# Sparse attention with screened rows: the stages of a pair given steps of their own, and the screening scores issued twice

## The chip, the cores and the metric

The kernel runs on one core of one Trainium2 chip. A core has five engines with instruction streams of their own: PE (TensorE, matmuls; its weight loads are shown apart as PEld), DVE (VectorE), ACT (ScalarE), POOL (GpSimd) and SP (SyncE, which here only issues transfers). The metric is the time of one execution in device microseconds (us). "Clock" is the mean share of full speed that was granted to TensorE; the records know only 0.5 and 1.0. They begin with the first change of the clock; what comes before it is counted and printed as full speed, though it ran at half. (In the kernel before, until 31.4 us, the transposes of k start 213 ns apart; just after it, 109 ns.) So every mean clock here is a little too high: the 0.684 of before would be 0.65. A run is called slow when it is over 1.5% above the fastest run of the same kernel.

## The reference, cut to what matters

```python
# Q, K, V: (8, 12, 512, 64) float32; threshold = 0.1
scores  = np.einsum('bhqd,bhkd->bhqk', Q, K) / sqrt(64)
weights = softmax(scores)                          # max-subtracted, + 1e-10 in the sum
weights = np.where(weights > threshold, weights, 0)
weights = weights / (np.sum(weights, axis=-1, keepdims=True) + 1e-10)
return np.einsum('bhqk,bhkd->bhqd', weights, V)
```

With random data few rows have any weight above 0.1; all other output rows are zero. So the kernel screens every row cheaply in bf16, then computes exactly only rows that may pass.

## The kernel before

Two heads make a pair, and there are 48 pairs. The screening of a pair takes four steps, one for each block of 128 query rows; a step is numbered g, and `hp, qi = divmod(g, 4)`. The work of one pair, by engine:

- Transpose q and k on PE (fp32; PE writes into PSUM, a small memory of its own, from which the others copy), copy out on ACT, centre the keys on DVE.
- Four times: screening scores on PE (two heads, one matmul each), a row maximum on DVE for one head and a sum of exponentials on ACT for the other (in one of the four, the sum on ACT for both).
- Flag the rows (DVE), rank them by matmuls with a triangle of ones (PE), make slot keys (DVE), turn these into row indices (PE), gather the selected query rows (DVE adds an offset, POOL issues).
- For the selected 128 slots: split the two heads' rows (DVE), transpose them (PE), fp32 scores (PE), exponential (ACT), mask (DVE), transpose the mask (PE), copy it out (DVE), multiply by V (PE), normalise (DVE, ACT), scatter to the output (POOL). The output was filled with zeros before (SP).

The score matmul and the schedule of before:

```python
def do_qk(g):
    hp, qi = divmod(g, SO)
    for h2 in range(2):
        sc = spsum.tile([P, SO * P], f32)
        ps = slice(h2 * D, (h2 + 1) * D)          # head 0: rows 0-63, head 1: rows 64-127
        keep(nc.tensor.matmul(sc[:], lhsT=qk_t[hp][ps, 0, qi * P:(qi + 1) * P],
                              rhs=qk_t[hp][ps, 1, :], start=True, stop=True))
        sc_t[g, h2] = sc
# ...
for g in range((NP + 5) * SO):
    hp, qi = divmod(g, SO)
    # ... loads
    if g < G:
        do_qk(g)
    # ... qi == 0 and qi == 1 cut
    elif qi == 2:
        if has(hp - 1):
            do_idx(hp - 1)
        if g < G:
            do_screen(g)
        if has(hp - 1):
            do_gather(hp - 1)
        if has(nxt):
            do_kcentre(nxt)
        if has(hp - 3):
            do_xmask(hp - 3)
        if has(hp - 2):
            do_split(hp - 2)          # DVE, last in its step ...
        # ...
    else:
        if has(hp - 2):
            do_xtr(hp - 2)            # ... and PE needs it first in the next
        # ...
```

Every instruction keeps the order in which the program writes it, within its engine (`keep`). So a stage that stands early on one engine, and needs something late on another, stops the whole stream behind it.

The softmax here doesn't subtract the row's maximum and nothing guards it: scores larger than these inputs give would overflow.

Of the kernel before, what the change touches and what calls it, by code (L numbers as in the profile page):

```python
# [11 lines left out]
def kernel(  # L12
# [26 lines left out]
    nc = tc.nc  # L39
# [95 lines left out]
    nc.gpsimd.memset(cuts[:, 1, 0:SO - 1], CUT * CS / scale)  # L135
# [12 lines left out]
    ptpsum = ctx.enter_context(tc.tile_pool(name="ptpsum", bufs=1, space=bass.MemoryType.PSUM))  # L148
    mpsum = ctx.enter_context(tc.tile_pool(name="mpsum", bufs=2, space=bass.MemoryType.PSUM))
# [8 lines left out]
    qb_t, sq_t, nm_t = {}, {}, {}  # L158
# [25 lines left out]
    def do_qev(hp, sc):  # L184
        qk = tpool.tile([P, 2, SO * P], SCREEN)
        keep(nc.scalar.copy(qk[:, 0, :], sc[:]))  # L186
        qk_t[hp] = qk

    def do_kev(hp, sc):
        kt = ktpool.tile([P, SO * P], f32)  # L190
        ksum = small.tile([P, 1], f32)
        keep(nc.scalar.activation(kt[:], sc[:], ACTF.Copy, accum_out=ksum[:]))  # L192
        k_t[hp] = kt
        ks_t[hp] = ksum
# [12 lines left out]
    def do_norms(hp):  # L207
        nm = mpsum.tile([P, P], f32, name="sm")
        sq = sq_t.pop(hp)
        for which in range(2):  # L210
            for r in range(SO):
                c = (which * SO + r) * 2
                keep(nc.tensor.matmul(nm[:, c:c + 2], lhsT=sq[:, which, r * P:(r + 1) * P], rhs=heads[:],
                                      start=True, stop=True))
        nm_t[hp] = nm
# [6 lines left out]
    def do_qk(g):  # L222
        hp, qi = divmod(g, SO)
        for h2 in range(2):
            sc = spsum.tile([P, SO * P], f32)
            ps = slice(h2 * D, (h2 + 1) * D)
            keep(nc.tensor.matmul(sc[:], lhsT=qk_t[hp][ps, 0, qi * P:(qi + 1) * P],  # L227
                                  rhs=qk_t[hp][ps, 1, :], start=True, stop=True))
            sc_t[g, h2] = sc

    def do_screen(g):
# [5 lines left out]
        for h2 in range(2):  # L237
            sc = sc_t.pop((g, h2))
            if h2 == 0 or qi == SO - 1:
# [12 lines left out]
    def do_rank(hp):  # L252
        f = f_t[hp]
        rk = mpsum.tile([P, P], f32, name="sm")
# [18 lines left out]
    def do_idx(hp):  # L273
        oh = oh_t.pop(hp)[:].rearrange("p h s r -> p r (h s)")
        ix = mpsum.tile([P, P], f32, name="sm")
# [23 lines left out]
    def do_xtr(hp):  # L299
        xp = mpsum.tile([P, P], f32, name="sm")  # L300
# [29 lines left out]
    def do_xpt(hp):  # L330
        m = m_t.pop(hp)
        pt = ptpsum.tile([P, SO, P], bf16)
# [10 lines left out]
    def do_xpv(hp):  # L343
        pt, v_bf = pts_t.pop(hp), v_in.pop(hp)
        o = mpsum.tile([P, P], f32, name="sm")
# [10 lines left out]
    def do_xout(hp):  # L356
        o = o_t.pop(hp)
        rcp = small.tile([P, 1], f32)
        keep(nc.vector.tensor_scalar_add(rcp[:], o[:, D:D + 1], 1e-10))
        keep(nc.vector.reciprocal(rcp[:], rcp[:]))  # L360
        res = outp.tile([P, D], f32)
        keep(nc.scalar.activation(res[:], o[:, 0:D], ACTF.Copy, scale=rcp[:, 0:1]))  # L362
        keep(nc.gpsimd.indirect_dma_start(  # L363
            out=Or, out_offset=bass.IndirectOffsetOnAxis(ap=ix_t.pop(hp)[:, 0:1], axis=0),
            in_=res[:], in_offset=None, element_offset=hp * 2 * S * D, bounds_check=2 * S - 1, oob_is_err=False))
# [6 lines left out]
    do_qev(0, do_tr(q_in.pop(0)))  # L372
    do_kev(0, do_tr(k_in.pop(0)))
# [4 lines left out]
    def has(hp):  # L378
        return 0 <= hp < NP

    for g in range((NP + 5) * SO):
        hp, qi = divmod(g, SO)
        nxt = hp + 1
        if qi == 0 and has(hp + PRE):
            do_load(hp + PRE)
        if g < G:
            do_qk(g)
        if qi == 0:
            if has(hp - 1):
                do_flags(hp - 1)  # L390
                do_rank(hp - 1)
            if has(nxt):
                tr = do_tr(q_in.pop(nxt))
            if has(hp - 3):
                do_xqk(hp - 3)
            if g < G:
                do_screen(g)
            if has(nxt):
                do_qev(nxt, tr)
            if has(hp - 4):  # L400
                do_xptev(hp - 4)
            if has(hp):
                do_squares(hp)
        elif qi == 1:
            if has(nxt):
                tr = do_tr(k_in.pop(nxt))
            if has(hp - 4):
                do_xpv(hp - 4)
            if g < G:
                do_screen(g)  # L410
            if has(hp - 1):
                do_key(hp - 1)
            if has(nxt):
                do_kev(nxt, tr)
            if has(hp - 3):
                do_xexp(hp - 3)
        elif qi == 2:
            if has(hp - 1):
                do_idx(hp - 1)
            if g < G:  # L420
                do_screen(g)
            if has(hp - 1):
                do_gather(hp - 1)
            if has(nxt):
                do_kcentre(nxt)
            if has(hp - 3):
                do_xmask(hp - 3)
            if has(hp - 2):
                do_split(hp - 2)
            if has(hp - 4):  # L430
                do_xout(hp - 4)
        else:
            if has(hp - 2):
                do_xtr(hp - 2)
            if has(hp - 3):
                do_xpt(hp - 3)
            if has(hp):
                do_norms(hp)
            if has(hp + 2):
                do_vload(hp + 2)  # L440
            if g < G:
                do_screen(g)
            if has(hp - 2):
                do_xev(hp - 2)
            if has(hp):
                do_normev(hp)
# [10 lines left out]
    over_t = mpsum.tile([P, P], f32, name="sm")  # L457
# [9 lines left out]
    with tc.If(many > 0):  # L467
        with tc.For_i(0, NP, 1) as hp:
# [9 lines left out]
            for qi in range(SO):  # L478
                for h2 in range(2):
# [12 lines left out]
                    pt_ps = ptpsum.tile([P, SO, P], bf16, name="pt")  # L492
# [5 lines left out]
                    o = mpsum.tile([P, P], f32, name="sm")  # L498
# [47 lines left out]
```

## Time and profile before

| kernel before | |
|---|---|
| median of 4 runs | 483.32 us (480.74 to 484.42) |
| profiled span | 483.1 us |
| from the first screening scores to the end of the last | 8.2 to 453.6 us: 9.28 us a pair |
| mean distance of pairs 5 to 45 | 9.56 us |
| mean clock | 0.684 |

The first part of the page gives each engine's busy time:

```profile
PE 355.0 (73%) x2450; PEld 182.8 (38%) x2450; DVE 259.6 (54%) x729; ACT 261.3 (54%) x865; POOL 140.3 (29%) x172
```

No engine is near full, though PE, at 73%, looks like the one to watch. But part of that is the low clock: the same matmul is counted as longer. The view of windows over one pair (columns: window, its length, then busy time and instruction count of PE, PEld, DVE, ACT and POOL, the granted clock, the transfers' share, GB/s) says it for a pair that ran mostly at full clock:

```profile
69.00:78.30 9.30, 6.76 (x54) 3.15 (x53) 5.34 (x15) 5.30 (x18) 2.82 (x3) 0.87 0.53 117
```

Even there PE is idle 2.5 of 9.3 us.

### The profile page before, as it was taken

The page shows a single profiled execution, that of the slowest core. Times are in us where ns is not written, and L with a number is a line of the kernel's source. Part 1 is how long each engine was busy: PE and PEld are TensorE (multiplying, and loading weights), DVE is VectorE, ACT ScalarE, POOL GpSimd, SP SyncE. Part 2 cuts the span into 40 slices and gives each one's busy share as a digit, 9 for nine tenths or more (in the row PEclk, how much of TensorE's full clock was granted, in tenths as well). Part 3 has the DMA queues.
Part 4 walks back from the last instruction along what each step waited for, and adds up shares of the span by engine and source line. Part 5 has one row for each costly group of instructions (what it writes and reads, how often), then busy time and mean ns, then how long its engine had stood idle before and what let it go on. Part 6 is the DMA issues. An engine that isn't in the chain of part 4 may idle for free. (4 is left out here: it accounts for less than half of the span.)

```text
span 483.1 us, 7777 instructions
## 1 busy us (share of the span) xinstructions
PE 355.0 (73%) x2450; PEld 182.8 (38%) x2450; DVE 259.6 (54%) x729; ACT 261.3 (54%) x865; POOL 140.3 (29%) x172
## 2 busy tenths in 40 slices
PE   3878876887788678867886787688768867886861
PEld 2444333433434343434343433344343434343330
DVE  2565465556555654565456555555555565556540
ACT  3675465555645564556455556555565556564520
POOL 5122223223322332233223322432242233223221
PEclk9996667666766676677667666766676667666555
DMA  7994544454344435443544445445434441311000
GB/s 161 234 230 90 127 107 91 88 117 108 83 94 117 102 81 105 108 103 80 118 96 100 88 88 127 93 90 122 97 87 95 119 100 39 67 15 13 6 3 7
DMA packets 124461, 45.87 MB, mean 95 GB/s; under 512 B 104758, under 2 KB 118272, under 8 KB 124416
## 3 DMA queue, kind: packets, MB, share of 16 engines
q1 hardware_dynamic: 108288, 37.76, 30.3%
q0 software_dynamic: 16128, 7.57, 12.9%
q8 instruction: 21, 0.34, 0.3%
q14 instruction: 24, 0.20, 0.1%
HBM read 39.32 MB, written 14.16 MB: 111 GB/s over the span
## 5 line engine op out<-in xcount | busy, mean ns | idle before, releaser
L241 ACT ACTIVATE junk<-sc 128x512 bf16<-128x512 f32 x240 | 143.9, 603 | 77.5 <-PE sc L227 77.4
L244 DVE TENSOR_REDUCE stat<-sc 128x1 f32<-128x512 f32 x144 | 99.1, 688 | 123.0 <-PE sc L227 122.1
L284 POOL DMA_INDIRECT qsel<-in_Q_dram,idx x48 | 50.9, 1060 | 278.2 <-DVE idx L283 253.8
L227 PE MATMUL sc<-qk 64*128 64x512 bf16 x384 | 99.9, 515 | 2.0 <-DVE qk L197 1.8
L312 PE MATMUL sc<-kt,xq 128*128 128x512 f32 x96 | 91.6, 1058 | 0.0
L301 PE MATMUL sm<-identity_f,qb 128*128 128x128 f32 x48 | 18.4, 384 | 83.0 <-DVE qb L294 83.0
L363 POOL DMA_INDIRECT out_dram<-res,idx x48 | 48.9, 1019 | 54.7 <-ACT res L362 47.6
L362 ACT ACTIVATE res<-sm,rcp 128x64 f32<-128x64 f32 x48 | 15.1, 314 | 79.5 <-DVE rcp L360 72.9
L180 PE MATMUL sc<-identity_f,q_sb 128*128 128x128 f32 x192 | 49.4, 408 | 5.1 <-POOL heads L130 4.6
L241 ACT ACTIVATION_READ_ACCUMULATOR junk<-sc 128x1 f32 x240 | 50.6, 211 | 0.0
L180 PE MATMUL sc<-identity_f,k_sb 128*128 128x128 f32 x192 | 49.2, 406 | 2.0 <-DMA k_sb<-in_K_dram 1.9
L227 PEld LDWEIGHTS <-qk 64*128 64x128 bf16 x384 | 19.5, 98 | 73.4 <-issue 71.3
L186 ACT CAST qk<-sc 128x512 bf16<-128x512 f32 x48 | 28.1, 586 | 33.0 <-PE sc L180 33.0
L248 DVE TENSOR_TENSOR f<-stat,cuts 128x8 bf16<-128x8 f32 x48 | 8.0, 167 | 70.2 <-ACT junk L241 69.3
L301 PEld LDWEIGHTS sm<-identity_f,qb 128*128 128x128 f32 x48 | 7.3, 152 | 99.1 <-DVE qb L294 99.1
L180 PEld LDWEIGHTS sc<-identity_f,k_sb 128*128 128x128 f32 x192 | 31.7, 202 | 21.1 <-issue 21.1
L167 POOL DMA_DIRECT2D v_bf<-in_V_dram x48 | 37.4, 779 | 1.2 <-issue 1.2
L326 DVE SCALAR_TENSOR_TENSOR m<-e,tv 128x512 bf16<-128x512 f32 x48 | 36.1, 751 | 1.7
L192 ACT ACTIVATE kt<-sc 128x512 f32<-128x512 f32 x48 | 28.6, 596 | 13.9 <-PE sc L180 13.9
L180 PEld LDWEIGHTS sc<-identity_f,q_sb 128*128 128x128 f32 x192 | 32.0, 204 | 5.6 <-POOL heads L130 4.6
L204 DVE TENSOR_TENSOR sq<-qk 128x1024 bf16<-128x1024 bf16 x48 | 32.6, 679 | 0.0
L318 ACT ACTIVATE e<-sc 128x512 f32<-128x512 f32 x48 | 28.4, 593 | 6.6 <-PE sc L312 6.6
(64 smaller groups left out, 384.5 us busy)
## 6 DMA issues: line engine op xcount, KB each, us to landing
q_sb<-in_Q_dram SPq DMA_DIRECT2D x96, 128.0 KB, 3.2
k_sb<-in_K_dram SPq DMA_DIRECT2D x96, 128.0 KB, 2.9
out_dram<-zero SPq DMA_DIRECT2D x48, 256.0 KB, 3.1
v_bf<-in_V_dram POOLq DMA_DIRECT2D x48, 128.0 KB, 3.2
qsel<-in_Q_dram,idx POOLq DMA_INDIRECT x48, 2.5
out_dram<-res,idx POOLq DMA_INDIRECT x48, 2.2
```

The source lines that it names most:

```text
L167: keep(nc.gpsimd.dma_start(out=v_bf[:], in_=Vf[hp]))
L180: keep(nc.tensor.matmul(sc[:, r * P:(r + 1) * P], lhsT=src[:, r, :], rhs=identity_f32[:], is_transpose=True, start=True, stop=True))
L192: keep(nc.scalar.activation(kt[:], sc[:], ACTF.Copy, accum_out=ksum[:]))
L204: keep(nc.vector.tensor_tensor(out=sq[:], in0=qk[:], in1=qk[:], op=ALU.mult))
L227: keep(nc.tensor.matmul(sc[:], lhsT=qk_t[hp][ps, 0, qi * P:(qi + 1) * P], rhs=qk_t[hp][ps, 1, :], start=True, stop=True))
L241: keep(nc.scalar.activation(junk[:], sc[:], ACTF.Exp, scale=BETA * scale / CS, accum_out=stat[:, h2, qi:qi + 1]))
L244: keep(nc.vector.tensor_reduce(stat[:, h2, qi:qi + 1], sc[:], axis=AX.X, op=ALU.max))
L284: keep(nc.gpsimd.indirect_dma_start(out=qsel_bufs[hp % NS][:], out_offset=None, in_=Qr, in_offset=bass.IndirectOffsetOnAxis(ap=idx[:, 0:1] ...
L312: keep(nc.tensor.matmul(sc[:], lhsT=xq_t.pop(hp)[:], rhs=k_t.pop(hp)[:], start=True, stop=True))
L318: keep(nc.scalar.activation(e[:], xs_t.pop(hp)[:], ACTF.Exp, scale=scale, accum_out=sum1[:]))
L326: keep(nc.vector.scalar_tensor_tensor(out=m[:], in0=e[:], scalar=tv[:, 0:1], in1=e[:], op0=ALU.is_gt, op1=ALU.mult))
L363: keep(nc.gpsimd.indirect_dma_start(out=Or, out_offset=bass.IndirectOffsetOnAxis(ap=ix_t.pop(hp)[:, 0:1], axis=0), in_=res[:], in_offset=N ...
```

## The change

The intent was twofold. First, a pair's stages get steps of their own, so that PE never meets a stage in the same step as the stage that feeds it. Second, the screening scores are computed twice into the same buffer: the second copy writes the same numbers, and is there to keep TensorE busy enough for its full clock. The core of the diff:

```diff
@@ do_qk
-            keep(nc.tensor.matmul(sc[:], lhsT=qk_t[hp][ps, 0, qi * P:(qi + 1) * P],
-                                  rhs=qk_t[hp][ps, 1, :], start=True, stop=True))
+
+            for _ in range(2):
+                keep(nc.tensor.matmul(sc[:], lhsT=qk_t[hp][ps, 0, qi * P:(qi + 1) * P],
+                                      rhs=qk_t[hp][ps, 1, :], start=True, stop=True))
             sc_t[g, h2] = sc
@@ the loop
-    for g in range((NP + 5) * SO):
...          (the four branches by qi are gone)
+    PLAN = {
+        "pe": {-4: [do_ktr], -3: [do_qtr], 1: [do_norms], 5: [do_rank], 7: [do_idx], 12: [do_xtr],
+               14: [do_xqk], 18: [do_xpt], 20: [do_xpv]},
+        "act": {-4: [do_kev], -3: [do_qev], 2: [do_normev], 12: [do_xev], 15: [do_xexp], 21: [do_xout]},
+        "dve": {-2: [do_kcentre], 0: [do_squares], 4: [do_flags], 6: [do_key], 8: [do_gather],
+                11: [do_split], 17: [do_xmask], 19: [do_xptev], 21: [do_xrcp]},
+    }
+    LAST = 22
+
+    def run(engine, g):
+        for t in sorted(PLAN[engine], reverse=True):
+            hp, at = divmod(g - t, SO)
+            if at == 0 and 0 <= hp < NP and (hp > 0 or t >= 0):
+                for step in PLAN[engine][t]:
+                    step(hp)
+
+    for g in range(G + LAST):
...          (loads cut)
+        if g < G:
+            do_qk(g)
+        run("pe", g)
+        if g < G:
+            do_screen(g)
+        run("dve", g)
+        run("act", g)
```

A key of the plan is a step counted from the pair's first screening. Within a step the oldest pair's stage comes first (`reverse=True`). Beside that, the transposed mask's PSUM buffer joins the small PSUM pool (three shared buffers in place of two and one), k is transposed before q, and one of the four steps' exponential and maximum change places.

More of the change, by code (lines that the diff above doesn't have):

```diff
@@ L134 @@
     nc.gpsimd.memset(cuts[:], CUT_SUM)
-    nc.gpsimd.memset(cuts[:, 1, 0:SO - 1], CUT * CS / scale)
+    nc.gpsimd.memset(cuts[:, 1, :], CUT * CS / scale)
+    nc.gpsimd.memset(cuts[:, 1, 2:3], CUT_SUM)
     NS = 3
@@ L147 @@
     spsum = ctx.enter_context(tc.tile_pool(name="spsum", bufs=5, space=bass.MemoryType.PSUM))
-    ptpsum = ctx.enter_context(tc.tile_pool(name="ptpsum", bufs=1, space=bass.MemoryType.PSUM))
-    mpsum = ctx.enter_context(tc.tile_pool(name="mpsum", bufs=2, space=bass.MemoryType.PSUM))
+    mpsum = ctx.enter_context(tc.tile_pool(name="mpsum", bufs=3, space=bass.MemoryType.PSUM))
     junkp = ctx.enter_context(tc.tile_pool(name="junk", bufs=2))
@@ L157 @@
     xp_t, xq_t, xs_t, e_t, m_t, s_t, ptp_t, pts_t, o_t = {}, {}, {}, {}, {}, {}, {}, {}, {}
-    qb_t, sq_t, nm_t = {}, {}, {}
+    qb_t, sq_t, nm_t, rc_t, tr_t = {}, {}, {}, {}, {}
     def load_pair(q_sb, k_sb, hp):
@@ L182, in do_tr, with do_qtr, do_ktr, do_qev @@
         return sc
-    def do_qev(hp, sc):
+    def do_qtr(hp):
+        tr_t[hp, "q"] = do_tr(q_in.pop(hp))
+    def do_ktr(hp):
+        tr_t[hp, "k"] = do_tr(k_in.pop(hp))
+    def do_qev(hp):
+        sc = tr_t.pop((hp, "q"))
         qk = tpool.tile([P, 2, SO * P], SCREEN)
+        qk_t[hp] = qk
         keep(nc.scalar.copy(qk[:, 0, :], sc[:]))
-        qk_t[hp] = qk
-    def do_kev(hp, sc):
+    def do_kev(hp):
+        sc = tr_t.pop((hp, "k"))
         kt = ktpool.tile([P, SO * P], f32)
@@ L207, in do_norms @@
     def do_norms(hp):
-        nm = mpsum.tile([P, P], f32, name="sm")
+        nm = mpsum.tile([P, P], f32, name="sm", tag="sm")
         sq = sq_t.pop(hp)
@@ L238, in do_screen @@
             sc = sc_t.pop((g, h2))
-            if h2 == 0 or qi == SO - 1:
+            if h2 == 0 or qi == 2:
                 junk = junkp.tile([P, SO * P], bf16)
@@ L253, in do_rank @@
         f = f_t[hp]
-        rk = mpsum.tile([P, P], f32, name="sm")
+        rk = mpsum.tile([P, P], f32, name="sm", tag="sm")
         cnt = rk[:, 0:2 * SO].rearrange("p (h r) -> p h r", h=2)
@@ L274, in do_idx @@
         oh = oh_t.pop(hp)[:].rearrange("p h s r -> p r (h s)")
-        ix = mpsum.tile([P, P], f32, name="sm")
+        ix = mpsum.tile([P, P], f32, name="sm", tag="sm")
         for r in range(SO):
@@ L299, in do_xtr @@
     def do_xtr(hp):
-        xp = mpsum.tile([P, P], f32, name="sm")
+        xp = mpsum.tile([P, P], f32, name="sm", tag="sm")
         keep(nc.tensor.matmul(xp[:], lhsT=qb_t.pop(hp)[:].rearrange("p h d -> p (h d)"), rhs=identity_f32[:],
@@ L331, in do_xpt @@
         m = m_t.pop(hp)
-        pt = ptpsum.tile([P, SO, P], bf16)
+        sm = mpsum.tile([P, SO, P], bf16, name="smt", tag="sm")
+        pt = sm
         for kj in range(SO):
@@ L344, in do_xpv @@
         pt, v_bf = pts_t.pop(hp), v_in.pop(hp)
-        o = mpsum.tile([P, P], f32, name="sm")
+        o = mpsum.tile([P, P], f32, name="sm", tag="sm")
         for h2 in range(2):
@@ L354, in do_xpv, with do_xrcp @@
         o_t[hp] = o
-    def do_xout(hp):
-        o = o_t.pop(hp)
+    def do_xrcp(hp):
+        o = o_t[hp]
         rcp = small.tile([P, 1], f32)
@@ L360, in do_xout @@
         keep(nc.vector.reciprocal(rcp[:], rcp[:]))
+        rc_t[hp] = rcp
+    def do_xout(hp):
         res = outp.tile([P, D], f32)
-        keep(nc.scalar.activation(res[:], o[:, 0:D], ACTF.Copy, scale=rcp[:, 0:1]))
+        keep(nc.scalar.activation(res[:], o_t.pop(hp)[:, 0:D], ACTF.Copy, scale=rc_t.pop(hp)[:, 0:1]))
         keep(nc.gpsimd.indirect_dma_start(
             out=Or, out_offset=bass.IndirectOffsetOnAxis(ap=ix_t.pop(hp)[:, 0:1], axis=0),
-            in_=res[:], in_offset=None, element_offset=hp * 2 * S * D, bounds_check=2 * S - 1, oob_is_err=False))
+            in_=res[:], in_offset=None, element_offset=hp * 2 * S * D,
+            bounds_check=2 * S - 1, oob_is_err=False))
     PRE = 3
@@ L371 @@
         do_vload(hp)
-    do_qev(0, do_tr(q_in.pop(0)))
-    do_kev(0, do_tr(k_in.pop(0)))
+    do_ktr(0)
+    do_kev(0)
+    do_qtr(0)
+    do_qev(0)
     do_kcentre(0)
     G = NP * SO
-    def has(hp):
-        return 0 <= hp < NP
-    for g in range((NP + 5) * SO):
+    PLAN = {
[5 more added lines that the diff above has]
+    }
@@ L382 @@
+    LAST = 22
[6 more added lines that the diff above has]
+    for g in range(G + LAST):
         hp, qi = divmod(g, SO)
-        nxt = hp + 1
-        if qi == 0 and has(hp + PRE):
+        if qi == 0 and PRE <= hp + PRE < NP:
             do_load(hp + PRE)
+        if qi == 3 and hp + 2 < NP:
+            do_vload(hp + 2)
@@ L386 @@
         if g < G:
             do_qk(g)
-        if qi == 0:
-            if has(hp - 1):
-                do_flags(hp - 1)
-                do_rank(hp - 1)
-            if has(nxt):
-                tr = do_tr(q_in.pop(nxt))
-            if has(hp - 3):
-                do_xqk(hp - 3)
-            if g < G:
-                do_screen(g)
-            if has(nxt):
-                do_qev(nxt, tr)
-            if has(hp - 4):
-                do_xptev(hp - 4)
-            if has(hp):
-                do_squares(hp)
-        elif qi == 1:
-            if has(nxt):
-                tr = do_tr(k_in.pop(nxt))
-            if has(hp - 4):
-                do_xpv(hp - 4)
-            if g < G:
-                do_screen(g)
-            if has(hp - 1):
-                do_key(hp - 1)
-            if has(nxt):
-                do_kev(nxt, tr)
-            if has(hp - 3):
-                do_xexp(hp - 3)
-        elif qi == 2:
-            if has(hp - 1):
-                do_idx(hp - 1)
-            if g < G:
-                do_screen(g)
-            if has(hp - 1):
-                do_gather(hp - 1)
-            if has(nxt):
-                do_kcentre(nxt)
-            if has(hp - 3):
-                do_xmask(hp - 3)
-            if has(hp - 2):
-                do_split(hp - 2)
-            if has(hp - 4):
-                do_xout(hp - 4)
-        else:
-            if has(hp - 2):
-                do_xtr(hp - 2)
-            if has(hp - 3):
-                do_xpt(hp - 3)
-            if has(hp):
-                do_norms(hp)
-            if has(hp + 2):
-                do_vload(hp + 2)
-            if g < G:
-                do_screen(g)
-            if has(hp - 2):
-                do_xev(hp - 2)
-            if has(hp):
-                do_normev(hp)
@@ L456 @@
     nc.vector.tensor_reduce(over[:], most[:], axis=AX.X, op=ALU.max)
-    over_t = mpsum.tile([P, P], f32, name="sm")
+    over_t = mpsum.tile([P, P], f32, name="sm", tag="sm")
     nc.tensor.matmul(over_t[0:1, :], lhsT=over[:], rhs=identity_f32[:], start=True, stop=True)
@@ L491 @@
                                                    op0=ALU.is_gt, op1=ALU.mult)
-                    pt_ps = ptpsum.tile([P, SO, P], bf16, name="pt")
+                    pt_ps = mpsum.tile([P, SO, P], bf16, name="smt", tag="sm")
                     for kj in range(SO):
@@ L497 @@
                     nc.scalar.copy(pt[:], pt_ps[:])
-                    o = mpsum.tile([P, P], f32, name="sm")
+                    o = mpsum.tile([P, P], f32, name="sm", tag="sm")
                     for kj in range(SO):
```

## The prediction

> **What bounds the kernel now.** I read the page first, its forty slices and its groups:
>
> ```profile
> PE   3878876887788678867886787688768867886861
> ...
> PEclk9996667666766676677667666766676667666555
> ...
> L244 DVE TENSOR_REDUCE stat<-sc 128x1 f32<-128x512 f32 x144 | 99.1, 688 | 123.0 <-PE sc L227 122.1
> ...
> L227 PE MATMUL sc<-qk 64*128 64x512 bf16 x384 | 99.9, 515 | 2.0 <-DVE qk L197 1.8
> ...
> L301 PE MATMUL sm<-identity_f,qb 128*128 128x128 f32 x48 | 18.4, 384 | 83.0 <-DVE qb L294 83.0
> ```
>
> No engine is full: PE is busy 355 of 483 us (7.4 us for each of 48 pairs), VectorE 260 (5.4) and ScalarE 261 (5.4). VectorE's longest wait, 122 us, is for PE's scores; PE's longest, 83 us, is for VectorE (48 times 1.7 us, in front of the selected rows' transpose). So the engines wait for each other in turn, and PE runs at two thirds of its clock. The first full screening starts at 8.2 us and the last near 455 in the timeline: a pair takes (455 - 8.2)/48 = 9.3 us, and 28 us are tail.
>
> Next the timeline of PE alone, over a stretch in which the clock was full (until 75.8):
>
> ```profile
> 69.18 0.39 PE L227 MATMUL sc<-qk 64*128 64x512 bf16 x2
> 69.50 0.66 PE L180 MATMUL sc<-identity_f,k_sb 128*128 128x128 f32 x4
> 70.09 0.33 PE L349 MATMUL sm<-v_bf,pt 128*64 128x64 bf16 x8
> 70.35 0.25 PE L352 MATMUL sm<-ones_bf,pt 128*128 128x1 bf16 x4
> 70.53 0.39 PE L227 MATMUL sc<-qk 64*128 64x512 bf16 x2
> 70.91 0.29 PE L277 MATMUL sm<-row_no,oh 128*128 128x1 f16 x4
> 71.14 0.39 PE L227 MATMUL sc<-qk 64*128 64x512 bf16 x2
> 73.30 0.33 PE L301 MATMUL sm<-identity_f,qb 128*128 128x128 f32 x1 [1.78 <-DVE qb L294]
> 73.47 0.39 PE L334 MATMUL pt<-identity_bf,m 128*128 128x128 bf16 x4
> 73.92 0.34 PE L213 MATMUL sm<-heads,sq 128*128 128x2 bf16 x8
> 74.19 0.39 PE L227 MATMUL sc<-qk 64*128 64x512 bf16 x2
> 75.28 0.18 PE L256 MATMUL sm<-f,tri 128*128 128x8 bf16 x1 [0.70 <-ACT norms L218]
> 75.32 0.21 PE L258 MATMUL sm<-f,ones_bf 128*128 128x6 bf16 x3
> 75.39 0.73 PE L180 MATMUL sc<-identity_f,q_sb 128*128 128x128 f32 x4
> ```
>
> Columns: start, length, work, and in brackets PE's idle time and who ended it. Two stops of 1.8 and 0.7 us stand in each pair, because one step holds both a stage and the stage it needs (on VectorE the split waits behind four other stages of its own step). They also cost the clock, as the windows of 3.41 us show:
>
> ```profile
> 58.73:62.14 3.41, 3.41 (x24) 1.52 (x24) 1.19 (x3) 1.80 (x6) 0.00 (x0) 0.50 0.65 168
> 62.14:65.56 3.42, 1.80 (x21) 1.20 (x20) 2.46 (x8) 1.56 (x8) 1.28 (x2) 0.50 0.37 80
> 65.56:68.97 3.41, 3.07 (x13) 1.40 (x12) 1.69 (x4) 2.05 (x8) 1.55 (x2) 0.50 0.32 41
> 68.97:72.38 3.41, 2.56 (x27) 1.30 (x26) 2.54 (x8) 2.42 (x8) 0.30 (x1) 1.00 0.71 190
> 72.38:75.79 3.41, 1.72 (x23) 1.28 (x24) 1.84 (x7) 2.24 (x9) 2.38 (x3) 1.00 0.21 48
> ```
>
> The second number is PE's busy time, the third from the end the granted clock. A window with PE busy throughout (58.73) did not raise the clock of the next; one with 3.07 us (65.56) did. So busy time is not what decides. I counted columns streamed instead (a scores pair in two row halves as 512, a 128-column fp32 transpose as 256, since they stand 0.109 us apart, the fp32 scores of selected rows as 4 x 512). Over all windows of the trace, cold ones above about 3150 columns are followed by a full clock and those below are not; full-clock windows with 3300 or more stay, those with 2130 or less fall. A pair has 7300 such columns, some 2700 for each window of 9.3 us of pair: just too few, so the clock goes up and down once in each pair.
>
> **What the Trainium skill says.** "TensorE: Matmul & The Clock Gate", Part 1 (The HAM clock gate): PE is throttled to half its clock unless a free-running window of about 3.4 us was busy. The trace agrees: the granted share is only ever 0.5 or 1.0, in stretches of 3.413 us or multiples. Part 2 there (Back-to-back issue gap) gives N/2.4 + 2.5 ns for a matmul of N columns warm and N/1.2 ns cold: 0.216 and 0.427 us for 512. Part 3 (Packing small matmuls) says that matmuls on different row groups overlap; here the two heads of a scores pair, in rows 0-63 and 64-127, take 0.39 us together, as long as one. Part 4 (PE-mode transpose) says that transposes do not count as busy for the gate; my count fits the trace only with them in, so I go by the trace.
>
> **The change part by part.** (1) The stages of a pair get steps of their own, each a step or more after what feeds it; the order of the built program confirms it, and VectorE's and ScalarE's instructions are the same in number and size (one reduction and one exponential change places). Gone are PE's stops before the split rows' transpose (1.7 us) and before the rank (0.3 to 0.7).
> (2) Each scores matmul is issued twice. The order on PE is head 0, head 0, head 1, head 1. The second of head 0 needs the same rows as the first, so waits 0.213 us; the first of head 1 overlaps it; the second of head 1 comes 0.213 later. A step costs 0.43 us more at full clock, 1.7 us a pair (0.85 and 3.4 at half).
> (3) PSUM: the transposes' own buffer joins the small pool, three shared instead of two and one; still five score buffers.
>
> PE's work of a pair at full clock, from start to next start above: scores 4 x (0.32 + 0.43) = 3.0; two transpose groups 2 x 0.59 = 1.18; selected scores half of their cold 1.85 = 0.93 (estimate); selected transposes 0.17 + 0.30; weights by V 0.26 + 0.18; norms 0.27; rank 0.11; index 0.23. Sum 6.6 us. VectorE needs 5.4, ScalarE 5.4. So PE is the bound if its clock is full, and the work is hidden behind it.
>
> What waits are left? I laid the steps out by the built waits. Step 1 holds on VectorE: reduce (scores end 0.81 after the step starts, +0.06 semaphore, 0.69), two reciprocal parts 0.31, threshold 0.17, mask 0.75: mask ready at 2.8. PE has by then done step 1 (scores 0.75, rank 0.11, norms 0.27, transposes 0.59) and step 2's scores (0.75) = 2.5, and waits 0.3 for the mask. Step 3: reduce and copy of the transposed mask end at 2.0; PE gets there at 0.98 + 0.75 = 1.7, waits 0.3. The score buffers come free a step ahead. Pair: 6.6 + 0.6 = 7.2; I add 0.3 for waits not seen, 7.5.
>
> The clock: a pair has 9500 columns now even with a half-row matmul as 256; in 7.5 us that is 4300 for each window, and the thinnest stretch (steps 3 and 0) still has 3800, over the 3300 that held. At half clock a pair would take some 11.7 us with 2760 on average, but the windows with the selected scores reach 3200 and more, so it gets warm in the first pairs that have all stages, and stays.
>
> Time: 8.2 + 48 x 7.5 + 28 (the tail is the same chain, with a few steps more in name) = 396; 2 for the cold start: **398 us**, 0.83 of the time before.
>
> **The rivals.** (a) *The clock stays low or falls often.* Then doubled scores are pure cost: 11.7 us a pair, 600 us. For it: only a count of columns says otherwise, and half-row matmuls could count for less. Against: every window count above. 5 in 100. (b) *The doubled matmuls don't overlap* (head 1 waits for both of head 0): 0.21 more a step, 8.3 a pair, 435 us. Against: the 4 ns between the heads' starts today. (c) *The output's queues become the bound.* A scatter waits for a zero fill to land and the next fill for that scatter: POOL 1.0 + landing 2.2 + issue 0.6 + landing 3.1 = 6.9 us a round, and the index of a later pair waits for the scatter's buffer. Hidden at 9.3 us, it is close to 7.5; with landings of 4 us, 8 us a pair, 420. (d) *VectorE and ScalarE turn out the bound* at 5.4 each: this would need PE's 6.6 to be too high; with no waits at all 6.6 gives 355.
>
> **Range and chances.** The spread of (b), (c) and a clock lost now and then is upward, that of no waits downward: 375 to 435. Faster by over 2% 0.93; within 2% 0.03; slower 0.04, nearly all of it (a).
>
> **What would show it.** Right: granted clock over 0.9 from about 50 us to the last scores; the scores group 768 matmuls, four in about 0.8 us; a pair in 7.2 to 7.8 us; PE's wait before the split rows' transpose gone, and its longest waits 0.3 us on the mask and the copied transposes. Wrong: a clock of 0.5 in long stretches (a); four scores in 1.0 us (b); PE, VectorE or POOL waiting for fills or scatters in each pair (c); PE idle over 1 us a pair on anything else.

## The result, and the profile after

| | before | after |
|---|---|---|
| median (range), 4 runs each | 483.32 us (480.74 to 484.42) | 352.38 us (351.61 to 353.02) |
| ratio of fast runs, 95% interval | | 0.7296 (0.7260 to 0.7332) |
| clock of the profiled run | 0.684 | 0.961 |
| mean distance of pairs 5 to 45 | 9.56 us | 6.58 us |
| before the first scores, after the last | 8, 30 us | 9, 28 us |

A ratio here is the mean time of one kernel's fast runs over that of the other's of the same rounds, so it is not quite the ratio of the medians. The changed kernel is 27% faster; the predicted 398 us and its range of 375 to 435 were both too high.

The page of the kernel after, first its busy times, PE's slices and the clock:

```profile
PE 284.2 (81%) x2834; PEld 135.5 (39%) x2834; DVE 262.9 (75%) x729; ACT 259.1 (74%) x865; POOL 154.9 (44%) x173
...
PE   2698988888888988888988888888888888887650
...
PEclk9998999999999999999999999999999999999655
```

PE issues 384 more matmuls (2834 against 2450) and is still busy 71 us less, because the clock record now shows full speed from 33.3 to 326.8 us without a break. DVE and ACT have the busy time they had, in a span 132 us shorter. Next the groups that answer to those of before (columns: line, engine, operation, output from inputs, shapes, count; busy us, mean ns of one; idle time just before them and who ended it):

```profile
L237 PE MATMUL sc<-qk 64*128 64x512 bf16 x768 | 118.6, 385 | 0.7 <-ACT qk L194 0.7
...
L345 PE MATMUL smt<-identity_bf,m 128*128 128x128 bf16 x192 | 19.7, 227 | 26.5 <-DVE m L336 26.0
...
L360 PE MATMUL sm<-v_bf,pt 128*64 128x64 bf16 x384 | 16.1, 205 | 17.9 <-DVE pt L351 17.9
```

The scores take 118.6 us busy for 768 where 384 took 99.9. In the listing that keeps shapes apart, the selected rows' transpose, which had waited 83 us for the split rows, waits almost nothing:

```profile
L311 PE MATMUL sm<-identity_f,qb 128*128 128x128 f32 x48 | 15.1, 315 | 1.7 <-DVE qb L304 1.7
```

PE's longest waits are now for the mask (L336) and for the copy of the transposed mask (L351). The timeline of PE over one pair, from one mask's transposes to the next:

```profile
150.11 0.40 PE L345 MATMUL smt<-identity_bf,m 128*128 128x128 bf16 x4 [0.50 <-DVE m L336]
150.34 1.08 PE L322 MATMUL sc<-kt,xq 128*128 128x512 f32 x2
151.35 0.61 PE L237 MATMUL sc<-qk 64*128 64x512 bf16 x4
151.89 0.29 PE L287 MATMUL sm<-row_no,oh 128*128 128x1 f16 x4
152.12 0.61 PE L237 MATMUL sc<-qk 64*128 64x512 bf16 x4
153.11 0.33 PE L360 MATMUL sm<-v_bf,pt 128*64 128x64 bf16 x8 [0.38 <-DVE pt L351]
...
153.63 0.60 PE L180 MATMUL sc<-identity_f,k_sb 128*128 128x128 f32 x4
154.16 0.61 PE L237 MATMUL sc<-qk 64*128 64x512 bf16 x4
...
155.58 0.61 PE L237 MATMUL sc<-qk 64*128 64x512 bf16 x4
156.69 0.40 PE L345 MATMUL smt<-identity_bf,m 128*128 128x128 bf16 x4 [0.50 <-DVE m L336]
```

Two things are to be seen. From the mask's transposes at 150.11 to the next at 156.69 a pair takes 6.58 us, with two waits in it. And a step's four score matmuls stand 0.54 us from what follows them (151.35 to 151.89), not the 0.75 us that the prediction had worked out. The windows view of a stretch of one whole period, 6.58 us, around the same pair:

```profile
149.97:156.55 6.58, 5.70 (x59) 2.72 (x59) 5.45 (x16) 5.34 (x20) 3.17 (x4) 1.00 0.70 148
```

PE is busy 5.70 us and idle 0.88, which is the two waits of the timeline, 0.50 and 0.38.

**Why a step costs 0.54.** The single records of the step at 151.35 settle it. The program issues head 0 twice, then head 1 twice. In the trace the four start at 0, 7, 226 and 233 ns, and last 386, 386, 376 and 376 ns. The second to start carries the wait for ScalarE, which only head 1's first matmul has; the two that start last carry the semaphore updates, which only each head's second copy has. So the first copy of head 1 ran beside the first copy of head 0, ahead of head 0's second copy, which stands before it in the program. At half clock, in the first step at 9.05 us, the same pattern shows with 401 ns between the two couples. The doubling thus costs one matmul's time a step, 0.22 us, and not two. Nor did the compiler put the copies in that order: in most steps head 1 starts 3 to 4 ns after head 0 where one copy of head 0 stands before it in the program (the kernel before, and experiment 4), 6 to 7 ns with two copies and 10 ns with three (experiment 3). It comes up later by some 3 ns for each copy written ahead of it, and passes those that have to wait. Three of the 192 steps, all before 27 us, did start in the written order.

### The profile page after: what moved, and what is told of

It is laid out like the page before. It is cut to its first block, busy times and chain, and to the rows that moved or that the text cites. A ratio compares the mean times of both kernels' runs of the same rounds, so it can differ in the third digit from the quotient of the medians.

```text
span 350.6 us, 8644 instructions
## 1 busy us (share of the span) xinstructions
PE 284.2 (81%) x2834; PEld 135.5 (39%) x2834; DVE 262.9 (75%) x729; ACT 259.1 (74%) x865; POOL 154.9 (44%) x173
## 5 line engine op out<-in xcount | busy, mean ns | idle before, releaser
L294 POOL DMA_INDIRECT qsel<-in_Q_dram,idx x48 | 62.1, 1294 | 139.3 <-DVE f L258 124.6
L237 PE MATMUL sc<-qk 64*128 64x512 bf16 x768 | 118.6, 385 | 0.7 <-ACT qk L194 0.7
L322 PE MATMUL sc<-kt,xq 128*128 128x512 f32 x96 | 54.4, 650 | 0.0
L345 PE MATMUL smt<-identity_bf,m 128*128 128x128 bf16 x192 | 19.7, 227 | 26.5 <-DVE m L336 26.0
L336 DVE SCALAR_TENSOR_TENSOR m<-e,tv 128x512 bf16<-128x512 f32 x48 | 36.1, 752 | 1.7
L180 PE MATMUL sc<-identity_f,k_sb 128*128 128x128 f32 x192 | 29.9, 280 | 9.0 <-DMA k_sb<-in_K_dram 9.0
L205 DVE TENSOR_SCALAR qk<-kt,ksum 128x512 bf16<-128x512 f32 x48 | 30.3, 632 | 6.7 <-ACT kt L200 6.7
L180 PE MATMUL sc<-identity_f,q_sb 128*128 128x128 f32 x192 | 31.8, 290 | 0.0
L360 PE MATMUL sm<-v_bf,pt 128*64 128x64 bf16 x384 | 16.1, 205 | 17.9 <-DVE pt L351 17.9
L345 PEld LDWEIGHTS <-m 128*128 128x128 bf16 x192 | 11.2, 99 | 48.9 <-DVE m L336 47.9
L360 PEld LDWEIGHTS <-pt 128*64 128x64 bf16 x384 | 10.6, 113 | 42.5 <-DVE pt L351 39.5
```

The lines of the kernel that those rows point to most:

```text
L180: keep(nc.tensor.matmul(sc[:, r * P:(r + 1) * P], lhsT=src[:, r, :], rhs=identity_f32[:], is_transpose=True, start=True, stop=True))
L205: keep(nc.vector.tensor_scalar(qk_t[hp][:, 1, :], k_t[hp][:], CS, ks_t.pop(hp)[:, 0:1], op0=ALU.mult, op1=ALU.subtract))
L294: keep(nc.gpsimd.indirect_dma_start(out=qsel_bufs[hp % NS][:], out_offset=None, in_=Qr, in_offset=bass.IndirectOffsetOnAxis(ap=idx[:, 0:1] ...
L322: keep(nc.tensor.matmul(sc[:], lhsT=xq_t.pop(hp)[:], rhs=k_t.pop(hp)[:], start=True, stop=True))
L336: keep(nc.vector.scalar_tensor_tensor(out=m[:], in0=e[:], scalar=tv[:, 0:1], in1=e[:], op0=ALU.is_gt, op1=ALU.mult))
L345: keep(nc.tensor.matmul(pt[:, kj, :], lhsT=m[:, kj * P:(kj + 1) * P], rhs=identity_bf[:], is_transpose=True, start=True, stop=True))
```

## The experiments

The theory after the result: the plan brings nearly all of the gain, by removing PE's stops and by that lifting the clock; the doubling costs 0.22 us a step, since the two heads' matmuls run beside each other copy by copy, and the miss of the prediction is that 0.22 for 0.43. The rivals: that the plan alone falls back to a low clock and the doubling is what lifts it; that the heads do run in series and something else became shorter; and that the output's round of scatter and zero fill sets the pair. All twelve kernels gave the right result. The runs of before beside them had medians of 481.39 to 482.35 us.

**1. The plan with single scores.**

```diff
-            for _ in range(2):
+            for _ in range(1):
```

> The new plan with each scores matmul issued once. Theory A (the clock follows the columns streamed in each window of 3.41 us, threshold near 3150): a pair has 7400 columns and PE needs about 4.9 us for it, so the pair is set by VectorE and its waits at 5.9 to 6.2 us, some 4200 columns for each window, and the clock stays over 0.9; time 315 to 335 us, so the doubling would be pure cost. Theory B (the doubling is what holds the clock): the granted clock falls to 0.5 for long stretches, mean 0.5 to 0.75, PE's pair at half clock is 8.5 to 9 us, time 400 to 450 us.

Measured: 340.20 us (337.17 to 349.17, 5 runs), ratio 0.7010 (0.6957 to 0.7063), clocks 0.907 to 0.953; the runs of 344.25 and 349.17 count as slow. The plan alone is faster than plan and doubling together (0.7296) by 4%. (It is 5 us above the range of theory A, and far from theory B.) Undisturbed pairs take 6.13 us, 0.45 less than with the doubling: of the 4 x 0.22 = 0.88 us that PE saves, half turns into longer waits. But the clock is no longer sure; the page shows two dents:

```profile
PEclk9996999957999999999999985999999999995555
```

They are falls at 67.2 us for 13.7 us and at 203.8 us for 10.2 us. The timeline ahead of the first shows a stop:

```profile
64.72 1.02 POOL L377 DMA_INDIRECT out_dram<-res,idx  x1 [3.60 <-ACT junk L251]
...
66.89 0.22 DVE L293 TENSOR_SCALAR idx<-sm,slot_base 128x1 int32<-128x1 f32 x1 [1.04 <-DMA out_dram<-res,idx]
...
67.24 0.19 PE L266 MATMUL sm<-f,tri 128*128 128x8 bf16 x1 [0.76 <-DVE f L258]
```

DVE's index addition wants a buffer that a scatter still reads, waits 1.04 us for that scatter to land, and PE waits 0.76 us in its turn. The window of the clock record that ends there holds 2775 streamed columns (the count is explained after the experiments), under the prediction's limit of 3150; undisturbed ones hold 3724 or more; the clock falls, and then takes up to 13.7 us to come back. That this wait is the cause is argued here from its place; experiment 6 takes it away. So neither side was wholly right: the plan does lift the clock by itself, and the doubling does make it steady (the four runs of the changed kernel lie within 0.4%), at a price above what it brings.

**2. The kernel before with double scores.** The same doubling in `do_qk` of the kernel before, and nothing else.

> The kernel before with each scores matmul issued twice and nothing else. Theory A: the two stops of 1.8 and 0.7 us in each pair stay, the windows with them hold under 2500 columns, so the clock still falls once in each pair; mean clock 0.68 to 0.8, and the extra 0.2 to 0.4 us a step is partly paid: 470 to 510 us. Theory B: the clock goes to over 0.9 by the doubling alone and the time falls to 420 to 450 us.

Measured: 497.65 us (463.59 to 509.86, 4 runs), so unclear; clocks 0.859, 0.761, 0.693 and 0.691 from the fastest run to the slowest. Three of the four count as slow, and the fastest, with the highest clock, is 4% below the median of before: the doubling alone is no sure gain. The profiled run keeps a high clock for half its time and loses it:

```profile
PEclk9988888979888888976766667766667666676655
```

A pair takes 8.08 us where the clock is full, and 10.24 us once it has settled into one fall a pair, which is three windows of 3.413 us. The 8.08 tells two parts of the gain apart, taken in this order (doubling first, then the plan; the other order would share it out otherwise): at full clock with double scores, the old schedule takes 8.08 and the plan 6.58. So 1.5 of the 2.98 us a pair between the kernels is stops that the plan removes; the other 1.5 is what a full clock brings, less the cost of the doubling.

**3. Three copies.** `range(3)` in the changed kernel.

> The changed kernel with each scores matmul issued three times: measures what one further issue costs. If the two heads' copies run beside each other whatever their order in the program, a step costs 0.21 us more, a pair 0.85 us less what the waits for VectorE absorb (up to 0.88): 352 to 393 us, four steps' scores at 0.75 us each. If copies of one head run one after the other with only one overlap, 0.43 more a step, 1.7 a pair: 395 to 435 us. Clock over 0.9 in both.

Measured: 370.98 us (369.84 to 372.62, 4 runs), ratio 0.7704 (0.7652 to 0.7756), clock 0.966. A step's scores take 0.76 us to the next start (151.47 to 152.23), again 0.22 more, and a pair takes 7.04 us, 0.46 more. One, two and three copies give 0.32, 0.54 and 0.76: each copy costs one matmul, for both heads together. A third copy buys no clock.

**4. The order head 0, head 1, head 0, head 1 written in the program.**

```diff
-        for h2 in range(2):
-            sc = spsum.tile([P, SO * P], f32)
-            ps = slice(h2 * D, (h2 + 1) * D)
-            for _ in range(2):
-                keep(nc.tensor.matmul(sc[:], ...
-            sc_t[g, h2] = sc
+            sc_t[g, h2] = spsum.tile([P, SO * P], f32, name="sc")
+        for _ in range(2):
+            for h2 in range(2):
+                ps = slice(h2 * D, (h2 + 1) * D)
+                keep(nc.tensor.matmul(sc_t[g, h2][:], ...
```

> The changed kernel with the four scores matmuls of a step in the program order head 0, head 1, head 0, head 1 in place of 0, 0, 1, 1. If PE already runs the copies of the two heads beside each other (the trace after shows starts 7, 226 and 233 ns after the first): the same time within 0.5%. If the order in the program mattered: faster by about 0.2 us a step, 35 us in all.

Measured: 351.57 us (351.33 to 351.79, 4 runs), ratio 0.7299 (0.7257 to 0.7342), pairs of 6.58 us. Nothing changes, as it must if PE had already run the copies in this order; the spacing of the starts (3 ns here, 7 ns there) shows that the two programs did differ.

**5. The heads forced into series.** A matmul of one column that uses all 128 rows, ahead of head 1's scores, in the first column of its buffer (the scores then overwrite it).

```diff
+            if h2 == 1:
+                keep(nc.tensor.matmul(sc[:, 0:1], lhsT=tri[:], rhs=ones_bf[:, 0:1], start=True, stop=True))
```

> The changed kernel with one 128-row matmul of a single column between the two heads' scores matmuls (it writes what the next overwrites), so that the heads cannot run beside each other. Measures what the doubled issue would have cost in series: scores of a step 0.95 to 1.05 us from start to next start in place of 0.54, PE's work of a pair 1.6 to 2.0 us more, of which the waits of 0.9 us for VectorE absorb up to half: 400 to 440 us, clock over 0.9. If the overlap of the heads is not what made the doubling cheap: 352 to 365 us.

Measured: 468.02 us (444.31 to 490.92, 4 runs), clocks 0.961 to 0.967. The total missed the expected 400 to 440 us, and it is no measure of the disputed cost: in the profiled run (451.55 us) the clock stays at half until 78.2 us, with pairs of 13.85 us in place of 8.11. (The record's 0.962 counts that stretch as full speed; 0.875 would be right.) Without it that run would have taken some 420 us, an estimate from these two numbers. That a longer or shorter start also spreads the other three runs is likely, but they left no trace. At full clock the timeline is:

```profile
200.77 0.60 PE L238 MATMUL sc<-qk 64*128 64x512 bf16 x2
201.30 0.18 PE L236 MATMUL sc<-ones_bf,tri 128*128 128x1 bf16 x1
201.41 0.60 PE L238 MATMUL sc<-qk 64*128 64x512 bf16 x2
201.95 0.33 PE L361 MATMUL sm<-v_bf,pt 128*64 128x64 bf16 x8
```

One head's copies now come before the other's, and a step takes 1.18 us (200.77 to 201.95) at full clock instead of 0.54, more than the 0.95 to 1.05 that was expected; a pair takes 8.11 us. Two copies of one head alone take 0.53 (200.77 to 201.30), as long as the four of both heads in the changed kernel. That is what a series looks like (the separator's 0.11 us included), and the changed kernel doesn't look like it. The rival of heads in series has fallen.

**6. Single scores, with the index in a pool of its own.** The wait of experiment 1 taken away: `idx` comes from a pool of eight buffers instead of the shared pool of four.

```diff
+    idxp = ctx.enter_context(tc.tile_pool(name="idx", bufs=8))
-        idx = small.tile([P, 1], i32)
+        idx = idxp.tile([P, 1], i32)
```

> The new plan, scores issued once, and the index tile in a pool of its own with eight buffers in place of four shared ones. In the run with single issue the clock fell where VectorE's index addition waited 1.0 and 1.2 us for a scatter to land (the scatter of four pairs earlier still held the index buffer); the window then held under 2800 columns. Theory A: without that wait no window falls under 3125 columns, the clock stays full until the last scores in every execution, a pair stays at 6.1 us, and the time is 328 to 337 us with a spread under 1%. Theory B (the falls come from thin work and chance, not from this wait): clock still 0.90 to 0.95 with falls of 7 to 14 us, 337 to 349 us as before.

Measured: 338.24 us (336.43 to 341.54, 4 runs), ratio 0.7017 (0.6958 to 0.7076), clocks 0.922 to 0.946. The wait is gone and the spread is smaller. In the profiled run, which counts as slow, the long falls in the middle are gone; a fall of 13.7 us at the start (34.5 us) and two of one window (3.4 us), at 181.3 and 263.2 us, stay. The ratio is that of experiment 1 (0.7010), and the fast runs have the clocks of its fast runs (0.940 to 0.946, there 0.941 to 0.953): no gain in time is shown. So that buffer probably caused the two long falls of that trace; it was not the only cause of falls.

**7. Stages shifted to meet the two waits that are left.** From kernel 6, each stage that PE waits for is given one step more.

```diff
-               ... 1: [do_norms], 5: [do_rank], ... 18: [do_xpt], 20: [do_xpv]},
+               ... 5: [do_rank, do_norms], ... 19: [do_xpt], 21: [do_xpv]},
-        "act": {... 2: [do_normev], ... 21: [do_xout]},
+        "act": {... 6: [do_normev], ... 22: [do_xout]},
-        "dve": {... 0: [do_squares], ... 19: [do_xptev], 21: [do_xrcp]},
-    LAST = 22
+        "dve": {... 3: [do_squares], ... 20: [do_xptev], 22: [do_xrcp]},
+    LAST = 23
```

> As the run with the index pool, and the plan moved so that no stage on PE has its VectorE stage in the step before with other VectorE work in front: transposes of the mask at step 19, their copy 20, weights by V 21, reciprocal and output 22; squares at 3, norms 5 and 6. Theory A: the waits of PE for mask and copy (together 1.2 us a pair with single issue) go, and the pair falls from 6.1 to what VectorE needs, 5.5 to 5.8 us: 305 to 320 us. Theory B: VectorE's and ScalarE's own work (5.4 each) with waits in turn already sets the 6.1: 325 us or more, with VectorE's idle time unchanged.

Measured: 372.92 us (368.50 to 377.10, 4 runs), clocks 0.831 to 0.860, pairs of 7.22 us. This missed: 10% slower than kernel 6 by the medians (9% by the two fast runs of the four), not faster. In the profile PE waits 44 us for the split rows, against 4 us in kernel 6. The likely way, read from the trace and not tested apart from the other moves: the output comes a step later, so its scatter stands later on POOL, and the gather of the next rows behind it; the clock falls along with it. Removing a wait by moving a stage had made a longer one elsewhere.

**8. Single scores, the zero fill issued for two pairs at a time.** A scatter waits for the last zero fill to land, and a fill for the last scatter, since both write the output. From kernel 6:

```diff
-        nc.sync.dma_start(out=Oz[hp], in_=zero[:])
+        if hp % 2 == 0:
+            nc.sync.dma_start(out=Oz[hp:hp + 2].rearrange("n p f -> p n f"),
+                              in_=zero[:].unsqueeze(1).to_broadcast([P, 2, 2 * SO * D]))
```

> The run with single issue and the index pool, with the zero fills of the output issued for two pairs at a time. Each scatter waits for the last fill to land and each fill for the last scatter; in the single-issue runs the round is 2.9 us from scatter to fill and 3.2 from fill to scatter, 6.1 us, as long as the pair. Theory A (this round is what makes the single-issue pair late now and then and thins a window): with one round for two pairs the hiccups go, the clock is full from the third or fourth window to the last scores, spread under 1%; the pair stays near 6.0 us because PE still waits 0.6 us each for mask and copy: 325 to 334 us. Theory B: still falls of the clock, 336 to 345 us.

Measured: 334.32 us (331.66 to 337.23, 4 runs, the slowest of them counted as slow), ratio 0.6925 (0.6871 to 0.6979), clocks 0.940 to 0.952. In the profiled run the clock is full from 34.9 to 301.2 us without a fall, and every pair takes 6.13 us. The medians differ from kernel 6 by 1.2%, and the intervals overlap, so the gain in time is not sure; the missing falls are what the profile shows.

**9. The same fill in the shifted kernel.** Kernel 7 with the edit of kernel 8.

> The shifted plan, single issue, with fills for two pairs at a time. In the shifted run the scatter waited up to 5 us for a fill and the gather behind it on the same queue was late, so PE waited for the split rows (1.3 us a pair). Theory A (that round of 6.6 to 7.7 us was its bound, not the plan): the pair falls from 7.3 to 5.5 to 5.8 us, 303 to 320 us, PE's waits for split rows under 0.3 us a pair. Theory B (the shifted plan is itself worse): over 350 us again, with the same waits.

Measured: 360.57 us (357.96 to 363.11, 4 runs), ratio 0.7488 (0.7432 to 0.7545), clocks 0.849 to 0.881. Better than 372.92, but still far behind kernel 8, so the shift is bad by itself too. One scatter of it shows the round of fill and scatter at its longest:

```profile
201.56 1.02 POOL L380 DMA_INDIRECT out_dram<-res,idx  x1 [5.59 <-DMA out_dram<-zero]
```

POOL stood idle 5.59 us for a fill; at the same time, DVE waited 3.92 us for gathered rows, and PE 4.17 us for DVE.

**10. The same fill in the changed kernel.** The kernel after, double scores, with the edit of kernel 8 alone.

> The changed kernel itself (scores issued twice) with fills for two pairs at a time. If its pair of 6.58 us is PE's work of 5.75 and its 0.9 us of waits for VectorE, as I read it: the same time, 348 to 354 us. If the round of scatters and fills (3.2 + 3.0 to 3.3 us in its trace) already bounds it: faster, 325 to 342 us.

Measured: 353.66 us (350.97 to 355.56, 4 runs), ratio 0.7341 (0.7289 to 0.7394), against 0.7296 without it. The same within the intervals: at 6.58 us a pair the round of fill and scatter does not bind. In the trace of the changed kernel a scatter at 149.84 us is followed by a fill at 153.48 and a scatter at 156.43, and that scatter is released by its own data, not by the fill.

**11. Single scores, the youngest pair first on PE and ScalarE.** From kernel 8. In the plan the oldest pair's stage comes first within a step; on these two engines that stage is the one that waits for DVE (the mask, the copied transposes), so it holds up younger stages whose inputs are ready. With the order turned round, it comes last.

```diff
-        for t in sorted(PLAN[engine], reverse=True):
+        for t in sorted(PLAN[engine], reverse=(engine == "dve")):
```

> The run with single issue, index pool and fills by two, and within a step PE and ScalarE take the youngest pair's stage first (selected scores before the mask's transposes, key and split transposes before weights by V), so that the two waits of 0.6 us a pair for mask and copy run behind other PE work. Theory A (those waits are what is left between PE's 4.9 us and the pair of 6.13): the pair falls to what VectorE and ScalarE need, 5.4 to 5.8 us, 300 to 320 us, clock over 0.93. Theory B (the waits come back elsewhere, or the round of scatter and fill binds first): 6.0 us or more, 328 us or more.

Measured: 317.12 us (314.89 to 319.46, 4 runs), ratio 0.6567 (0.6517 to 0.6617), clocks 0.909 to 0.926. This beats both kernels: 34% less than before, and 10% less than the change. Pairs take 5.2 to 5.4 us undisturbed, 5.90 in the mean, since the clock falls five times in the profiled run after the start, for 3.4 or 6.8 us each. The two waits have gone from PE's timeline in the undisturbed pairs; the multiplication by V and the mask's transposes stand without a bracket:

```profile
143.24 0.33 PE L363 MATMUL sm<-v_bf,pt 128*64 128x64 bf16 x8
...
146.15 0.39 PE L348 MATMUL smt<-identity_bf,m 128*128 128x128 bf16 x4
```

(The lines are 348 and 363 in this kernel, 345 and 360 in the changed one.)

**12. The same with double scores.**

> The same with the scores issued twice. PE needs 5.75 us a pair then. Theory A: the pair falls from 6.58 to 5.8 to 6.0 us, 315 to 328 us, steadier than the single-issue run but no faster. Theory B (the waits come back elsewhere): 6.4 us or more, 340 us or more.

Measured: 323.76 us (323.06 to 326.74, 6 runs), ratio 0.6715 (0.6672 to 0.6758), clocks 0.958 to 0.985. The clock is full from 19.6 to 299.5 us without a fall, and a pair takes 6.00 us, 0.10 more than with single scores and their falls; by the ratios 2% is lost. Here too the doubling gives a steady clock and costs more than it gives.

**The clock by columns.** The prediction's count was made again for each window of 3.413 us of the clock record, from 7 us on, in all fourteen traces. A matmul counts its output columns, twice if it is in float32, times the share of the 128 rows that it uses; they are spread from its start on, 512 over 0.219 us at full clock and over twice that at half. The prediction's own limit, 3150 columns, which it had from the kernel before alone, then tells whether the next window is granted full clock or half in all 136 windows of that kernel and in all but 26 of 1309 of the other thirteen; the 26 lie between 2732 and 3292, some within 1% of the limit, where a few missing records can move a count. (Counting the half-width products with V at half their columns misses 46 in all.) Other measures do worse, even with the limit that suits each best: without the transposes 171 of all 1445 windows are missed, with columns not weighted by rows 90, with PE's busy time 189.

This fits experiment 5, which stays at half clock for so long: in the windows between 13 and 75 us PE is busy throughout, but one head's scores use half of the rows, and the windows hold 1542 to 3003 columns. It also suggests what the doubling buys. Between 90 and 195 us the thinnest window of experiment 1 holds 3724 columns, that of the changed kernel 4269: further from the limit, so that a stop should cost it the clock less easily (argued from the counts, not tested apart).

## Why the prediction was wrong

- **The failed step.** "The second of head 0 needs the same rows as the first, so waits 0.213 us; the first of head 1 overlaps it; the second of head 1 comes 0.213 later. A step costs 0.43 us more at full clock, 1.7 us a pair". It took the program's order for the order in which PE runs matmuls on different rows. Head 1's first copy ran beside head 0's first copy, 219 ns ahead of head 0's second, and the second copies ran beside each other. A step costs 0.22 us more, 0.88 a pair. Three copies (0.76 a step), the order written out (no change) and the heads forced into series (1.18 a step) all agree with that.
- **The plan.** Its part (1) had each stage a step or more after what feeds it. That holds for PE's stages, and the stops that it said would go are gone; four stages of ScalarE still follow their feeder within a step.
- **The sum.** By starts in the timeline, PE's work of a pair is scores 4 x 0.54 = 2.16 (predicted 3.0), selected scores 1.01 (0.93), the k and q transposes 0.53 and 0.57 (1.18), selected transposes 0.15 and 0.23 (0.47), weights by V 0.26 and 0.11 (0.44), norms 0.20 (0.27), rank 0.11 (0.11) and index 0.23 (0.23): 5.56 in place of 6.6. Most of the difference is the scores term.
- **The waits.** Predicted were 0.3 for the mask, 0.3 for the copied transposes and 0.3 not seen. The two waits are the right two, but longer: from the end of the scores' share to the next start 0.45 and 0.57, in all 1.02. No third one is there. Work and waits make 5.56 + 1.02 = 6.58, against 7.5; the excess of 0.92 x 48 = 44 us takes 398 to 354, and 352.4 was measured.
- **The bound.** "PE is the bound if its clock is full" is right only with its waits in: PE is busy 5.70 of 6.58 us. That half of the saved or added matmuls is absorbed by the waits (0.45 us a pair for 0.88 of work) shows that the stream of PE and what DVE hands back set the pair together.
- **The clock and the ends.** Right: full from 33 us to the last scores, as the count of columns said (its "once in each pair" for the clock of before is four times in five pairs, in the clock record); the stop before the split rows' transpose is gone; the start was 9 us (predicted 8.2 and 2 cold) and the tail 28 (28).
- **The rivals.** (a), a low clock, did not come. (b) had the mechanism and the wrong direction: it feared that the heads would overlap less than was assumed, and they overlapped more. (c), the round of fills and scatters, does not bind here (run 10), but it makes itself felt in faster kernels (runs 8 and 9). (d) gave "with no waits at all 6.6 gives 355"; the number is close to the result, by chance: the work was 5.56, and the waits 1.02.
- **What was not asked.** The prediction treated the doubling as the price of the clock. Run 1 shows that the plan alone holds the clock for most of the time, at 340.20 us.

Left open: the change also shared PSUM buffers, turned k and q round and swapped one maximum with a sum; every experiment on the plan has these in it, so what they bring is not known. What the falls of the clock in run 11 start from, each in its turn, was not followed; nor was a version looked for that has a single copy and no falls at 5.3 us a pair.

## What to carry to other kernels

Take the time of two matmuls that can overlap from the trace, start to next start, and try the doubled or tripled form before counting on an order: what is written as A, A, B, B may run as A and B, A and B. A schedule that keeps every stage of PE a step away from its feeder can be worth more for the clock than filler work; try the schedule without the filler too, and try which pair's stage comes first within a step, which gave another 5% here with one changed argument. Moving a stage later to spare one wait also moves everything that is queued behind it, here the scatter and the next gather.

## What the Trainium skill lacked or had wrong

- "TensorE: Matmul & The Clock Gate", Part 3 (Packing small matmuls) says that matmuls start and end strictly in program order. Matmuls on rows 0 to 63 and 64 to 127 written as head 0, head 0, head 1, head 1 started at 0, 7, 226 and 233 ns, the second of them being head 1's first: it started 219 ns ahead of a matmul that stands before it in the program. Written as head 0, head 1, head 0, head 1, the kernel takes the same time (351.57 against 352.38 us), and with three copies of head 0 written first, head 1 starts 10 ns after the first of them.
- The same page, Part 1 (The HAM clock gate), says that a window of about 3.4 us must be busy, but gives no measure of busy; only Part 4 (PE-mode transpose) says that transposes do not count in the same way. In these runs a window with PE busy for all of its 3.41 us did not raise the clock (58.73 us in the kernel before, and all from 13 to 75 us in experiment 5), and a count of streamed columns, weighted by the rows used, with a limit of 3150 a window, is right for 1419 of 1445 windows of fourteen kernels. Against Part 4, the transposes have to be in it: without them 171 windows are missed in place of 26.
